# A two-layer RWKV-7 and sparse-attention kernel: the decay's first column set by VectorE, four pairs' products and the first inverses issued later, and one unit's bonus sums in another phase

## The chip, the cores and the metric

The kernel runs on one core of a Trainium2 chip. The metric is the time of one execution in microseconds (us) as the device reports it, and the median of several executions is compared. The engines are TensorE (PE; its weight loads are shown as PEld), VectorE (DVE), ScalarE (ACT), GpSimd (POOL) and SyncE (SP), which here only issues transfers. Each engine works through its own list of instructions in order, and waits at an instruction until the semaphores that it needs have been raised.

## The reference

The reference runs 256 tokens of width 2048 through two layers. The first is an RWKV-7 mixer, the second an attention layer over compressed, selected and windowed keys. The change touches the first layer alone. Cut to what matters, it computes per head of 64:

```python
kk = kk / jnp.maximum(jnp.sqrt(jnp.sum(kk * kk, axis=-1, keepdims=True)), 1e-12)
k = k * (1.0 + (a - 1.0) * k_a)

def step(S, inp):                       # over the 256 tokens
    r_t, w_t, k_t, v_t, a_t, b_t = inp
    sa = jnp.einsum('bhvk,bhk->bhv', S, a_t)
    S = S * w_t[:, :, None, :] + sa[..., None] * b_t[:, :, None, :] + v_t[..., None] * k_t[:, :, None, :]
    return S, jnp.einsum('bhvk,bhk->bhv', S, r_t)

bonus = jnp.sum((rh * kh * r_k).astype(jnp.float32), axis=-1, keepdims=True) * vh
o = (o + bonus.reshape(B, T, D)) * jax.nn.silu(z)
return o.astype(u.dtype) @ w_o, v
```

There are 32 heads, so 16 pairs of heads (128 rows, one per partition) and 8 units of two pairs.

## The kernel before

All large products are made with 32-bit numbers split in a high and a low half: ACT rounds (`whi`, L207), DVE subtracts (`wlo`, L192), and TensorE makes three matmuls for one. The weights stream through five raw buffers; their loads stand in SP's list (L179).

The recurrence over tokens is done in four chunks of 64. Inside a chunk it needs the inverse of a triangular matrix for each head, which is made in advance.

**Up to about 335 us** the projections run: values, then blocks of z (`phase_z`) and keys (`phase_k`, one for each pair) in the order z0, k0 to k7, z1, k8 to k11, z2, k12 to k15, z3. Beside them run generators, which give back a time after which they want to be continued; a small scheduler in Python (`Sched`) counts the time of the matmuls that it has emitted and continues them when due. In this part the order of each engine's list is then set once more by a list scheduler, which simulates the program and takes what is ready.

- `stage_k(j)` makes for pair j the decayed keys in the buffer `sp` (three of them): `pp` (the running decay, whose first column of every chunk is 1), `at`, `BK` and `kr`. POOL sets the first column (L758), makes a power for the norm (`rnt`, L747), which ACT spreads (`rnx`, L753) and TensorE turns (L756), and makes the products `BK` (L775, L776). DVE makes `nk`, `at` and `an` (L768 to L770). The buffer is stored to DRAM (`spd`, L778). Eight small matmuls (L784) give the matrix to be inverted; ACT copies it (L788), and SP stores it (`abdd`, L796). Pair j starts after the matrix of pair j - 2 is issued.
- `stage_t(b)` inverts the matrices of pairs 8b to 8b + 7, on DVE almost alone: it loads them (`invA`, L819), sets the diagonal of `invT` (L828), copies the first entries below it (L830), doubles the size in steps of 2 and 4 (L849 to L860) and then of 8 and 16 (L868, L873), and stores the result from POOL (L894, L900). Inverse 0 runs beside the projections, inverse 1 in the scan.

**From about 335 to 550 us** the scan runs; there all lists stand in the order of the code. For each unit U of 8 there are 12 phases: chunk c = 0 to 3, step p = 0 to 2. Step 0 makes `px` (L1105, and L1121 with the state S), which ACT copies to `X`; step 1 makes `pu` (L1128), step 2 the output and the next state (L1134, L1137), which DVE copies or adds (L1140, L1142). In between the phases TensorE makes the projection r and the output projection (`fill`; L1257 to L1259 are r's), and the next unit's preparations (A: L1088, L1090; masks on DVE: L1096; G: L1055; Y: L1064; B: L1074). The bonus sums (L1116) are 16 matmuls with a moving operand of two columns that add up `mb` over a head.

After 550 us come the key and value projections, the attention and the output; the change leaves them alone.

Of the kernel before, what the change touches and what calls it, by code (L numbers as in the profile page):

```python
# [13 lines left out]
OP = mybir.AluOpType  # L14
# [6 lines left out]
NCH = T // CH  # L21
# [197 lines left out]
def hybrid_kernel(ctx: ExitStack, tc: tile.TileContext, a: dict, out: bass.AP):  # L219
    nc = tc.nc  # L220
    V, S, G, PE = nc.vector, nc.scalar, nc.gpsimd, nc.tensor
# [36 lines left out]
    def accp(name="acc"):  # L258
        n = turn.get(name, 0)
        turn[name] = n + 1  # L260
        b = role[name]
        return psum.tile([128, 512], F32, name=f"bank{b[n % len(b)]}", bufs=1)
# [27 lines left out]
    for q in range(4):  # L290
        for k in (4 * q, 4 * q + 2):
            first, second = [W.add(wv[(k + i) * 128:(k + i + 1) * 128, 0:1024].rearrange("p (u c) -> p u c", u=2), 1, False)
                             for i in range(2)]
# [158 lines left out]
    pp = accp("pp")  # L452
# [262 lines left out]
    def stage_k(j):  # L715
        PE, V, S, G = Ranked(nc.tensor, "skPE"), Ranked(nc.vector, "skE"), Ranked(nc.scalar, "skE"), Ranked(nc.gpsimd, "skE")
        yield lambda: j in kdone and (j < KLAG or (j - KLAG) in a1done)
        tmp = lambda name, bufs=2: kph.tile([128, T], F32, name=name, bufs=bufs)
        sp = kph.tile([128, SPW], F32, name="sp", bufs=3)
        abs_ = tmp("abs")  # L720
        BK = sp[:, 0:512].rearrange("p (c x t) -> p c x t", c=NCH, x=2)
        pp = sp[:, 512:512 + NCH * (CH + 1)].rearrange("p (c t) -> p c t", c=NCH)
        kr = sp[:, SPW - 512:SPW - 256]
        at = sp[:, SPW - 256:]
        w2t = w2[j // 2]
        sc = (j % 2) * 128
        la = accp("la")
        PE.matmul(la[:, :256], w2t[:, 0, sc:sc + 128], hw, start=True, stop=True)
        PE.matmul(la[:, 256:], w2t[:, 1, sc:sc + 128], ha, start=True, stop=True)
        sch.t += 860  # L730
        pk = kps.pop(j)
        ksb = tmp("ksb")
        sqk = tmp("t1")
        S.activation(ksb, pk, AF.Copy)
        S.activation(sqk, pk, AF.Square, scale=KK[:, j:j + 1])
        rn = accp("rn")
        for tt in range(2):
            PE.matmul(rn[:, 256 + 2 * tt:258 + 2 * tt], sqk[:, tt * 128:(tt + 1) * 128], C("bo"), start=True, stop=True)
        sch.t += 430
        yield 400.0  # L740
        sst = kph.tile([128, 2, 2], F32, name="sst", bufs=2)
        rnt = kph.tile([128, 2, 2], F32, name="rnt", bufs=2)
        thw, tha = tmp("thw"), tmp("tha")
        S.activation(thw, la[:, :256], AF.Tanh, scale=0.5, bias=W0H[:, j:j + 1])
        S.activation(tha, la[:, 256:], AF.Tanh, scale=0.5, bias=A0H[:, j:j + 1])
        V.tensor_scalar(sst, rn[:, 256:260].rearrange("p (a b) -> p a b", a=2), 1e-24, None, op0=OP.max)
        G.tensor_tensor(rnt, sst, half[:, 0:4].rearrange("p (a b) -> p a b", a=2), op=OP.pow)  # L747
        S.activation(thw, thw, AF.Copy, scale=0.5, bias=0.5)
        cum = tmp("cum")
        V.tensor_tensor_scan(cum, C("rst"), thw, 0.0, op0=OP.mult, op1=OP.add)  # L750
        yield 1000.0
        rnx = tmp("rnx")
        S.activation(rnx.rearrange("p (a b n) -> p a b n", a=2, b=2),  # L753
                     rnt[:, :, :, None].to_broadcast([128, 2, 2, 64]), AF.Copy)
        for tt in range(2):
            PE.transpose(rn[:, tt * 128:(tt + 1) * 128], rnx[:, tt * 128:(tt + 1) * 128], ident)  # L756
        sch.t += 215
        G.memset(pp[:, :, 0:1], 1.0)  # L758
        S.activation(pp[:, :, 1:], c3(cum), AF.Exp, scale=-DECAY)
        pinv = tmp("pinv")  # L760
        S.activation(pinv, cum, AF.Exp, scale=DECAY)
        an, f = tmp("an"), tmp("f")
        S.activation(an, tha, AF.Copy, scale=-0.5, bias=-0.5)
        S.activation(f, tha, AF.Identity, scale=KAH[:, j:j + 1], bias=KAM[:, j:j + 1])
        V.tensor_tensor(f, ksb, f, op=OP.mult)
        yield 800.0
        nk = tmp("nk")
        V.scalar_tensor_tensor(nk, ksb, KKN[:, j:j + 1], rn[:, :256], op0=OP.mult, op1=OP.mult)  # L768
        V.tensor_tensor(c3(at), c3(nk), pp[:, :, 0:CH], op=OP.mult)
        V.tensor_tensor(an, nk, an, op=OP.mult)  # L770
        S.activation(kr, f, AF.Copy, scale=RK[:, j:j + 1])
        yield 600.0
        for h in range(2):
            r = slice(64 * h, 64 * h + 64)
            G.tensor_tensor(BK[r, :, 1 - h, :], c3(an)[r], c3(pinv)[r], op=OP.mult)  # L775
            G.tensor_tensor(BK[r, :, h, :], c3(f)[r], c3(pinv)[r], op=OP.mult)  # L776
        yield 2500.0
        nc.sync.dma_start(spd[j], sp)  # L778
        ab = [accp("ab") for _ in range(2)]
        for c in range(NCH):  # L780
            q = slice(64 * (c % 2), 64 * (c % 2) + 64)
            for h in range(2):
                r = slice(64 * h, 64 * h + 64)
                PE.matmul(ab[h][q, c // 2 * 64:c // 2 * 64 + 64], c3(at)[r, c, :], BK[r, c, 1 - h, :], start=True, stop=True)  # L784
        sch.t += 350
        blocks = abs_.rearrange("p (n s) -> p n s", s=64)
        for h in range(2):
            S.activation(blocks[:, h::2], ab[h][:, :128].rearrange("p (n s) -> p n s", s=64), AF.Copy)  # L788
        for odd in range(2):
            for q in range(2):  # L790
                d = abdd[j // 8][q]
                n = 4 * (q + 1)
                dst = bass.AP(tensor=d.tensor, offset=d.offset + (j % 8 * 2 + odd) * n * 1024, ap=[[32, 32], [1024, n], [1, 32]])
                r0 = 64 * odd + 32 * q
                src = blocks[r0:r0 + 32].rearrange("p n (e s) -> p (n e) s", e=2) if q else blocks[r0:r0 + 32, :, 0:32]
                nc.sync.dma_start(dst, src)  # L796
        a1done.add(j)
# [12 lines left out]
    def stage_t(b):  # L810
        PE, V, S, G = Ranked(nc.tensor, "stE"), Ranked(nc.vector, "stE"), Ranked(nc.scalar, "stE"), Ranked(nc.gpsimd, "stE")
# [10 lines left out]
        if b:  # L822
            yield lambda: "inv" in phase_done
            V.memset(Tm, 0.0)
        else:
            yield 500.0
        flat = Tm.rearrange("p a b -> p (a b)")
        V.memset(flat[:, 0::33], 1.0)  # L828
        fa = A.rearrange("p a b -> p (a b)")
        V.tensor_copy(flat[:, 32::66], fa[:, 32::66])  # L830
        yield 1000.0

        pace = lambda ns: PACE[0] * (ns + 60.0) if b else 1.6 * (ns + 60.0)
# [6 lines left out]
        for lv in (2, 4):  # L840
            n = 32 // (2 * lv)
            m1 = M1.rearrange("p a b -> p (a b)")[:, :n * lv * lv].rearrange("p (n i j) -> p n i j", n=n, i=lv)
            m2 = M2.rearrange("p a b -> p (a b)")[:, :n * lv * lv].rearrange("p (n i j) -> p n i j", n=n, i=lv)
            x = X[:, :n * lv * lv].rearrange("p (n i j) -> p n i j", n=n, i=lv)
            sh = [128, n, lv, lv]
            for k in range(lv):
                colA = view(A, lv, k, n, 2 * lv, lv, 1).to_broadcast(sh)
                rowT = view(Tm, k, 0, n, 2 * lv, 1, lv).to_broadcast(sh)
                V.tensor_tensor(m1 if k == 0 else x, colA, rowT, op=OP.mult)  # L849
                if k:  # L850
                    V.tensor_tensor(m1, m1, x, op=OP.add)
                yield pace((1 if k == 0 else 2) * (1.1 * n * lv * lv + 60.0))
            for k in range(lv):
                colT = view(Tm, lv, lv + k, n, 2 * lv, lv, 1).to_broadcast(sh)
                rowM = m1[:, :, k:k + 1, :].to_broadcast(sh)
                V.tensor_tensor(m2 if k == 0 else x, colT, rowM, op=OP.mult)
                if k:
                    V.tensor_tensor(m2, m2, x, op=OP.add)
                yield pace((1 if k == 0 else 2) * (1.1 * n * lv * lv + 60.0))
            V.tensor_copy(view(Tm, lv, 0, n, 2 * lv, lv, lv), m2)  # L860
# [45 lines left out]
    H = lambda x, h: R[h ^ x]  # L906
# [200 lines left out]
    def phase(U, c, p):  # L1107
        uv, px, pu, pS = UV[U % 2], view(U, 0, 64), view(U, 64, 64), view(U, 128, 64)
        O = view(U, 192 + 64 * c, 64)
        st = SST[U][0] if c else None  # L1110
        if p == 0:
            if c == 0:
                for i in range(NCH):
                    for x, h in each:
                        o = x * 512 + 448 + 2 * i
                        PE.matmul(PBK[U][H(x, h), o:o + 2], mb[R[h], x, 64 * i:64 * i + 64], ones2[R[h]], start=True, **mm)  # L1116
            removal(U, c)
            if c:
                for k, o in enumerate((px, O)):
# [796 lines left out]
```

## Time and profile before

| | us |
|---|---|
| median of three runs | 1112.94 |
| lowest and highest | 1112.37, 1113.22 |
| the profiled execution | 1114.21 |
| its span, first to last instruction | 1112.4 |

The profile is of one execution, 1.27 us over the median. Rows of the timeline give start and duration in us, then engine, line, operation, what is written and read, the shape and a count; in square brackets stands how long the engine was idle before it, and what released it. Rows of waits give the waiting engine, its tile and line, the releaser, and the total, the number and the longest in us; "issue" is a wait for nothing that the profile shows. Rows by windows give for each stretch and engine the busy time and the number of instructions, then the clock that TensorE was granted, the busy share of the 16 transfer engines, and GB/s. A matmul with 32-bit operands that are not split shows twice, so the 16 of the bonus sums are 32 rows of the trace and 32 weight loads.

### The profile page before, as it was taken

To read this page: it belongs to the slowest core of one execution; us is meant where nothing else is said; L and a number is where in the kernel's file an instruction comes from. 1 tells how busy PE (TensorE), PEld (TensorE's weight loads), DVE (VectorE), ACT (ScalarE), POOL (GpSimd) and SP (SyncE) were. 2 spreads that over 40 slices of the span, in tenths; PEclk is the share of its full clock that TensorE was granted. 3 is DMA by queue.
4 is the path that set the end of the run, shared out by engine and by line. 5 is a ranking of instruction groups with operands and counts; after the bars stand their busy time and mean duration, and the time that the engine had idled before them with its cause. 6 is when DMAs were issued, how large, how long until landed. Compare 5 with 4: busy or idle time off the path is not lost.

```text
span 1112.4 us, 25288 instructions
## 1 busy us (share of the span) xinstructions
PE 1091.2 (98%) x9232; PEld 957.1 (86%) x9232; DVE 836.1 (75%) x1784; ACT 737.7 (66%) x1779; POOL 329.6 (30%) x409
## 2 busy tenths in 40 slices
PE   8999999999999999999999999999999999999997
PEld 7788899898889888999888888788989999988887
DVE  6999976779887796666667876665677988886564
ACT  7767877676775467776557766665666677775553
POOL 1300035424448456652200110100323324432012
PEclk9999999999999999999999999999999999999999
DMA  7458978877879777865578668675745354735762
GB/s 260 152 194 235 248 212 249 247 197 216 260 222 269 223 194 211 245 197 156 160 250 277 197 203 260 195 253 169 198 139 152 101 145 131 187 103 194 281 199 100
DMA packets 221965, 224.74 MB, mean 202 GB/s; under 512 B 48368, under 2 KB 173392, under 8 KB 221456
## 3 DMA queue, kind: packets, MB, share of 16 engines
q1 hardware_dynamic: 216512, 217.60, 66.1%
q0 software_dynamic: 4864, 4.92, 1.6%
q8 instruction: 73, 1.20, 0.4%
q10 hardware_dynamic: 464, 0.59, 0.1%
q14 instruction: 52, 0.43, 0.1%
HBM read 200.49 MB, written 22.58 MB: 201 GB/s over the span
## 4 chain that ended last, share of the span: by engine, by line
PE 54%; DVE 4%; DMA 2%; issue 1%; ACT 1%; POOL 0%; POOLq 0%; DVEq 0%; ACTq 0%
PE bank L619 9%; PE bank L617 9%; PE bank L616 9%; PE bank L1657 5%; PE bank L235 4%; PE bank L1658 3%; DVE wlo L192 2%; PE bank L1257 1%; PE pair L619 1%; PE pair L616 1%; PE pair L617 1%; PE bank L1258 1%; PE bank L1259 1%; PE bank L1223 1%; PE pair L1134 1%
## 5 line engine op out<-in xcount | busy, mean ns | idle before, releaser
L192 DVE TENSOR_TENSOR wlo<-wraw,whi 128x512 fp32r<-128x512 f32 (+2 forms) x616 | 440.3, 728 | 144.0 <-ACT whi L207 139.7
L207 ACT ACTIVATE whi<-wraw 128x512 fp32r<-128x512 f32 (+2 forms) x664 | 401.8, 618 | 179.5 <-PE bank L619 69.6
L192 POOL TENSOR_TENSOR wlo<-wraw,whi 128x512 fp32r<-128x512 f32 (+2 forms) x48 | 61.4, 1279 | 174.3 <-ACT whi L207 134.9
L617 PE MATMUL bank<-wlo,mh 128*128 128x512 f32 (+1 forms) x288 | 109.4, 381 | 0.8 <-DVE wlo L192 0.7
L617 PE MATMUL bank<-wlo,mhl 128*128 128x512 f32 (+2 forms) x288 | 107.9, 375 | 0.0
L619 PE MATMUL bank<-whi,ml 128*128 128x512 f32 (+1 forms) x288 | 107.9, 379 | 0.0
L619 PE MATMUL bank<-whi,mhl 128*128 128x512 f32 (+2 forms) x288 | 107.3, 373 | 0.0
L616 PE MATMUL bank<-whi,mhl 128*128 128x512 f32 (+2 forms) x288 | 99.5, 373 | 0.3 <-ACT Vt L1539 0.3
L616 PE MATMUL bank<-whi,mh 128*128 128x512 f32 (+1 forms) x288 | 92.0, 381 | 0.3 <-ACT whi L207 0.2
L1657 PE MATMUL bank<-mhl,whi 128*128 128x512 f32 x256 | 91.9, 397 | 0.0
L1257 PE MATMUL bank<-mhl,whi 128*128 128x256 f32 x256 | 78.6, 307 | 2.0 <-issue 2.0
L617 PE MATMUL bank<-wlo,kvh 128*128 128x512 f32 x192 | 76.0, 396 | 0.0
L634 PE MATMUL bank<-mh,whi 128*128 128x256 f32 x256 | 75.2, 294 | 0.4 <-ACT whi L207 0.4
L619 PE MATMUL bank<-whi,kvl 128*128 128x512 f32 x192 | 75.3, 392 | 0.0
L636 PE MATMUL bank<-mh,wlo 128*128 128x256 f32 x256 | 73.7, 290 | 0.0
L635 PE MATMUL bank<-ml,whi 128*128 128x256 f32 x256 | 73.4, 287 | 0.0
L1658 PE MATMUL bank<-mhl,wlo 128*128 128x256 f32 x256 | 73.0, 285 | 0.3 <-DVE wlo L192 0.3
L1259 PE MATMUL bank<-mhl,wlo 128*128 128x256 f32 x256 | 72.7, 284 | 0.1
L1258 PE MATMUL bank<-mhl,whi 128*128 128x256 f32 x256 | 72.7, 284 | 0.0
L616 PE MATMUL bank<-whi,kvh 128*128 128x512 f32 x192 | 66.7, 391 | 0.0
L617 PEld LDWEIGHTS bank<-wlo,mh 128*128 128x128 f32 x288 | 54.1, 188 | 11.5 <-DVE wlo L192 2.0
L619 PEld LDWEIGHTS bank<-whi,ml 128*128 128x128 f32 x288 | 54.2, 188 | 9.6
(384 smaller groups left out, 2746.4 us busy)
## 6 DMA issues: line engine op xcount, KB each, us to landing
wraw<-in_a_w_rkvz_dram SPq DMA_DIRECT2D x128, 512.0 KB, 5.1
wraw<-in_kv_w_dram SPq DMA_DIRECT2D x48, 512.0 KB, 4.4
wraw<-in_b_w_in_dram SPq DMA_DIRECT2D x40, 512.0 KB, 4.3
wraw<-in_a_w_o_dram SPq DMA_DIRECT2D x32, 512.0 KB, 4.9
wraw<-in_b_w_o_dram SPq DMA_DIRECT2D x32, 512.0 KB, 3.7
spd<-sp SPq DMA_DIRECT2D x16, 642.0 KB, 4.7
wraw<-in_b_w_in_dram SPq DMA_DIRECT2D x24, 384.0 KB, 3.2
wraw<-in_cmp_w_dram SPq DMA_DIRECT2D x16, 512.0 KB, 3.9
```

Source lines behind the costliest of these rows:

```text
L192: eng.tensor_tensor(lv, src, hv.bitcast(F32), op=OP.subtract)
L207: self.nc.scalar.activation(hv, src, AF.Copy)
L616: PE.matmul(o, mh[:, ts], wh[:, 0, :], start=k == ends[0], stop=False)
L617: PE.matmul(o, mh[:, ts], wl[:, 0, :], start=False, stop=False)
L619: PE.matmul(o, ml[:, ts], wh[:, 0, :], start=False, stop=k == ends[1])
L634: PE.matmul(o, wh[:, s, :], mh, start=k == 0 and first, stop=False, **kw)
L636: PE.matmul(o, wl[:, s, :], mh, start=False, stop=k == NK - 1, **kw)
L1257: PE.matmul(oo, wh[:, i, c], mh, start=k == 0 and x == 0, stop=False, **kw)
L1258: PE.matmul(oo, wh[:, i, c], ml, start=False, stop=False, **kw)
L1259: PE.matmul(oo, wl[:, i, c], mh, start=False, stop=k == NK - 1, **kw)
L1657: PE.matmul(o, wh[:, s, :], beside[("u", k)], start=k == 0, stop=False)
L1658: PE.matmul(o[:, :T], wl[:, s, :], mh, start=False, stop=k == NK - 1)
```

## The change

Five edits. In `stage_k` the first column of the decay is set by DVE instead of POOL and stands after `nk`, held in the program's order; the store of `sp` is issued before the pause ahead of the matrix products, not after it; and that pause is 9.5 us instead of 2.5 for pairs 8 to 11. In `stage_t` inverse 0 pauses 18 us instead of 0.5 before its first steps, and its first copy (now ahead of the diagonal) and its products of size 2 are held in the program's order. In `phase` the first unit's bonus sums are issued at the start of phase (1, 2), the sixth, and add to what stands there (`start=False`); those of the other units stay in phase (0, 0).

```diff
@@ stage_k
-        G.memset(pp[:, :, 0:1], 1.0)
         S.activation(pp[:, :, 1:], c3(cum), AF.Exp, scale=-DECAY)
...
         V.scalar_tensor_tensor(nk, ksb, KKN[:, j:j + 1], rn[:, :256], op0=OP.mult, op1=OP.mult)
+        tc.keep_in_program_order(V.memset(pp[:, :, 0:1], 1.0))
         V.tensor_tensor(c3(at), c3(nk), pp[:, :, 0:CH], op=OP.mult)
...
-        yield 2500.0
         nc.sync.dma_start(spd[j], sp)
+        yield 9500.0 if 8 <= j < 12 else 2500.0
@@ stage_t
         else:
-            yield 500.0
+            yield 18000.0
         flat = Tm.rearrange("p a b -> p (a b)")
+        fa = A.rearrange("p a b -> p (a b)")
+        first = V.tensor_copy(flat[:, 32::66], fa[:, 32::66])
+        if not b:
+            tc.keep_in_program_order(first)
         V.memset(flat[:, 0::33], 1.0)
-        fa = A.rearrange("p a b -> p (a b)")
-        V.tensor_copy(flat[:, 32::66], fa[:, 32::66])
...
-                V.tensor_tensor(m1 if k == 0 else x, colA, rowT, op=OP.mult)
+                first = V.tensor_tensor(m1 if k == 0 else x, colA, rowT, op=OP.mult)
+                if lv == 2 and not b:
+                    tc.keep_in_program_order(first)
...
-                V.tensor_tensor(m2 if k == 0 else x, colT, rowM, op=OP.mult)
+                first = V.tensor_tensor(m2 if k == 0 else x, colT, rowM, op=OP.mult)
+                if lv == 2 and not b:
+                    tc.keep_in_program_order(first)
@@ phase
+        if (c, p) == ((0, 0) if U else (1, 2)):
+            for i in range(NCH):
+                for x, h in each:
+                    o = x * 512 + 448 + 2 * i
+                    PE.matmul(PBK[U][H(x, h), o:o + 2], mb[R[h], x, 64 * i:64 * i + 64], ones2[R[h]], start=U > 0, **mm)
         if p == 0:
-            if c == 0:
-                for i in range(NCH):
...
             removal(U, c)
```

In the changed kernel the lines of this part have other numbers: `f` is L764, `nk` L767, the memset L768, the inverse's first copy L829 and its products of size 2 L851 and L860, r's matmuls L1263 to L1265, the bonus sums L1121.

How the lists of the engines differ is shown at three places. The first is POOL's list at the third to fifth pair of the keys, before and now:

```order
L747 TENSOR_TENSOR rnt<-sst,half 128x4
L758 MEMSET sp 128x4
L775 TENSOR_TENSOR sp<-an,pinv 64x4x64 x2
L776 TENSOR_TENSOR sp<-f,pinv 64x4x64 x2
L747 TENSOR_TENSOR rnt<-sst,half 128x4
L758 MEMSET sp 128x4
L775 TENSOR_TENSOR sp<-an,pinv 64x4x64 x2
```

```order
L747 TENSOR_TENSOR rnt<-sst,half 128x4
L775 TENSOR_TENSOR sp<-an,pinv 64x4x64 x2
L776 TENSOR_TENSOR sp<-f,pinv 64x4x64 x2
L747 TENSOR_TENSOR rnt<-sst,half 128x4
L775 TENSOR_TENSOR sp<-an,pinv 64x4x64 x2
```

The memsets are gone, and the products stand directly behind the power; the order of the rest is the same.

The second is the start of inverse 0, around the end of z1. DVE's list before, from a pair's `an` on:

```order
L770 TENSOR_TENSOR an<-nk,an 128x256
L192 TENSOR_TENSOR wlo<-wraw,whi 128x512 x8
L830 COPY invT<-invA 128x16
L849 TENSOR_TENSOR invM<-invA,invT 128x32
L849 TENSOR_TENSOR invX<-invA,invT 128x32
L192 TENSOR_TENSOR wlo<-wraw,whi 128x512
```

and now:

```order
L770 TENSOR_TENSOR an<-nk,an 128x256
L192 TENSOR_TENSOR wlo<-wraw,whi 128x512 x11
L691 TENSOR_TENSOR zth<-bank_2798,zth 128x512
L691 TENSOR_TENSOR zth<-bank_2799,zth 128x512
L192 TENSOR_TENSOR wlo<-wraw,whi 128x512
L829 COPY invT<-invA 128x16
L192 TENSOR_TENSOR wlo<-wraw,whi 128x512
L851 TENSOR_TENSOR invM<-invA,invT 128x32
```

The copy stands six rows later (four `wlo`, and z1's two products). On TensorE the eight matmuls of pair 8 (L784) stand 25 places later: behind the 1399th matmul of the list, not the 1374th, and behind the transposes of pair 9:

```order
L756 MATMUL bank_3303<-cst,rnx 128x128 x2
L634 MATMUL bank_3286<-mh,whi 128x256
L635 MATMUL bank_3286<-ml,whi 128x256
L636 MATMUL bank_3286<-mh,wlo 128x256
L784 MATMUL bank_3449<-sp 64x64
L784 MATMUL bank_3450<-sp 64x64
```

Those of pairs 9 and 10 stand 19 and 4 places later, those of pair 11 where they stood.

The third is the first unit's scan on TensorE. Before, at phase (0, 0):

```order
L1259 MATMUL bank_4693<-mhl,wlo 128x256
L1116 MATMUL pair_5093<-ones_4712,mb 64x2 x16
L1105 MATMUL pair_5093<-uv_4697,ama_4699 64x64 x4
L1257 MATMUL bank_4693<-mhl,whi 128x256
L1258 MATMUL bank_4693<-mhl,whi 128x256
```

and now, at phase (1, 2):

```order
L1061 MATMUL pair_5208<-Yb_4696,a_4559 64x32 x16
L1134 MATMUL pair_5093<-X,Yb_4560 64x64 x4
L1080 MATMUL bank_4692<-cst,spl_4695 128x128 x3
L1070 MATMUL pair_5208<-gs,t_4561 64x32 x16
L1121 MATMUL pair_5093<-ones_4712,mb 64x2 x16
L1140 MATMUL pair_5093<-uv_4697,amr_4701 64x64 x4
```

The sums now stand between the second unit's Y (L1070) and the output of the first unit's second chunk (L1140).

More of the change, by code (lines that the diff above doesn't have):

```diff
@@ L1110, in phase @@
         st = SST[U][0] if c else None
-        if p == 0:
-            if c == 0:
-                for i in range(NCH):
-                    for x, h in each:
-                        o = x * 512 + 448 + 2 * i
-                        PE.matmul(PBK[U][H(x, h), o:o + 2], mb[R[h], x, 64 * i:64 * i + 64], ones2[R[h]], start=True, **mm)
+        if (c, p) == ((0, 0) if U else (1, 2)):
[3 more added lines that the diff above has]
+                    PE.matmul(PBK[U][H(x, h), o:o + 2], mb[R[h], x, 64 * i:64 * i + 64], ones2[R[h]], start=U > 0, **mm)
+        if p == 0:
             removal(U, c)
```

## The prediction

> **What bounds the kernel now.** I read the page first, then who waited for whom, then short windows around the waits.
>
> ```profile
> PE 1091.2 (98%) x9232; PEld 957.1 (86%) x9232; DVE 836.1 (75%) x1784; ACT 737.7 (66%) x1779; POOL 329.6 (30%) x409
> ```
>
> TensorE is busy 98% of the span of 1112.4 us, so the change, which removes no matmul, can gain only from TensorE's idle time and slow time. These are the waits of TensorE that it can touch (total us, times, longest).
>
> ```profile
> PE bank L784 <- POOL sp L775: 2.1, 4, 0.7
> PE bank L1257 <- issue: 2.0, 1, 2.0
> PE bank L756 <- ACT rnx L753: 0.7, 1, 0.7
> PE bank L1090 <- issue: 0.7, 1, 0.7
> ```
>
> Together 5.5 us. Slow time shows in windows of 3.41 us (the granted clock stands behind POOL, ahead of the DMA share):
>
> ```profile
> core 0: us, PE busy (x) PEld busy (x) DVE busy (x) ACT busy (x) POOL busy (x), PEclk, DMA share, GB/s
> 244.65:248.06 3.41, 2.10 (x27) 1.69 (x26) 3.41 (x10) 1.29 (x4) 2.50 (x3) 1.00 0.49 158
> 248.06:251.47 3.41, 3.41 (x14) 3.23 (x15) 3.31 (x8) 2.99 (x8) 2.66 (x3) 0.50 0.92 297
> ...
> 360.70:364.11 3.41, 1.39 (x47) 1.30 (x46) 3.20 (x13) 0.80 (x2) 0.83 (x2) 1.00 1.03 283
> 364.11:367.53 3.42, 3.42 (x21) 3.08 (x21) 3.18 (x13) 0.78 (x3) 2.04 (x3) 0.50 1.12 308
> ...
> 370.94:374.35 3.41, 3.41 (x119) 2.90 (x119) 1.33 (x7) 2.58 (x8) 1.15 (x3) 1.00 0.94 284
> ```
>
> Twice a window in which TensorE did little (2.10 and 1.39 us busy) is followed by one at a clock of 0.50. The price of a slow window comes from the pace of like matmuls, full and slow:
>
> ```profile
> 238.08 0.28 PE L634 MATMUL bank<-mh,whi 128*128 128x256 f32 x1
> 238.20 0.28 PE L635 MATMUL bank<-ml,whi 128*128 128x256 f32 x1
> ...
> 248.59 0.41 PE L635 MATMUL bank<-ml,whi 128*128 128x256 f32 x1
> 248.80 0.41 PE L636 MATMUL bank<-mh,wlo 128*128 128x256 f32 x1
> ```
>
> 0.12 us from start to start against 0.21: a slow window loses 3.41 x (1 - 0.12/0.21) = 1.46 us. Both slow windows follow waits of the list above, so a wait there costs more than its length.
>
> [...]
>
> **Part 1: the first column's memset leaves POOL.** POOL is served in order.
>
> ```profile
> 171.90 0.42 DVE L770 TENSOR_TENSOR an<-nk,an 128x256 f32<-128x256 f32 x1
> ...
> 174.18 0.10 POOL L758 MEMSET sp<- 128x4 f32 x1 [5.07 <-DMA spd<-sp]
> ...
> 177.76 1.01 POOL L747 TENSOR_TENSOR rnt<-sst,half 128x4 f32<-128x4 f32 x1
> ...
> L758 POOL MEMSET sp<- x16: 100/105/108, 124.5 to 310.6; 128x4 f32 x16
> ...
>   DMA spd<-sp: 22.9, 8
> ...
> 355.46 0.09 DVE L828 MEMSET invT<- 128x32 f32 x1
> ```
>
> The memset belongs to a later pair than the products behind it, and waits 5.07 us for that pair's buffer to be stored, while the input of the products (`an`) is ready at 172.3. The products, the L784 matmuls and, through the late `rnt`, the L756 transposes wait for it: 0.7 us and one of the four L784 waits. All such waits of POOL are 22.9 us in 8 times, and leave with the memset. On DVE it stands behind `nk`, when ACT and POOL have long written the same buffer; it waits for nothing new. Its price is bounded by 0.105 us on POOL and the smallest DVE memset here, 0.09: 16 x 0.09 = 1.4 us of DVE in 200 us, of which 0.4 falls in the crowded stretch below.
>
> **Part 2: first inverses and products of pairs 8 to 11 later.**
>
> ```profile
> 227.52 1.15 ACT L690 ACTIVATE zth<-zth 128x512 f32<-128x512 f32 x2
> ...
> 228.29 0.18 DVE L830 COPY invT<-invA 128x16 f32<-128x16 f32 x1 [4.53 <-DMA invA<-abdd]
> ...
> 244.66 0.42 DVE L770 TENSOR_TENSOR an<-nk,an 128x256 f32<-128x256 f32 x1
> 245.15 2.31 POOL L775 TENSOR_TENSOR sp<-an,pinv 64x256 f32<-64x256 f32 x2 [4.13 <-DVE an L770]
> 246.38 0.45 PE L784 MATMUL bank<-sp 64*64 64x64 f32 x8 [0.63 <-POOL sp L775]
> ...
> 228.29:289.81 61.52, 58.56 (x132) 0.97 0.77 213
> 289.81 0.69 DVE L192 TENSOR_TENSOR wlo<-wraw,whi 128x512 fp32r<-128x512 f32 x1 [1.77 <-ACT whi L207]
> SPq L778 <- POOL sp L775: 9.6, 3, 3.8
> ```
>
> DVE stands 4.53 us for a load, and everything queued behind it is late for 60 us: DVE is busy 58.56 of 61.52 us until it is idle again (1.77 us at 288). Pair 8's `an` comes at 245.08, POOL's products end at 247.46, and TensorE, due at 245.75 (246.38 less 0.63), waits twice. Now the copy stands behind six more rows, the last the z products. Their input is ready at 228.67; two products and one `wlo` at 0.6 to 0.7 each put the copy at 230.6, 2.3 us later than before. But the six rows that stood behind it (some 4 us at 0.69) are then done: DVE's list is 4.0 - 2.3 = 1.7 us ahead (between 0, if inputs hold the rows up, and 4.53). Pair 8's chain also stands ahead of the inverse's wide rows, and its matmuls come 25 places later, 3 us at 0.12. So POOL is done ahead of TensorE, and the waits and the first slow window go.
>
> With part 1 this is 2.1 + 0.7 + 1.46 = 4.26 us. TensorE then runs 3.2 us earlier through this stretch (4.26 less the 1.1 of part 1), against 1.7 + 1.77 = 3.5 us that DVE has to give: just enough. I take off 0.7 us for waits that come into sight when TensorE is earlier (between 0 and 1.5): **3.5 us**.
>
> The stores of `sp` stand ahead of the yield, so SP blocks earlier on POOL; its longest such wait was 3.8 us, against five raw buffers of weights that are loaded ahead. I cost it at nothing; if that cover were gone, part of a 3.8 us wait would show on ACT's `whi`.
>
> **Part 3: the bonus sums of the first unit.**
>
> ```profile
> 361.26 0.64 PE L1116 MATMUL pair<-ones,mb 64*64 64x2 f32 x32
> 361.75 0.32 PE L1105 MATMUL pair<-uv,ama 64*64 64x64 f32 x8
> 364.10 0.37 PE L1257 MATMUL bank<-mhl,whi 128*128 128x256 f32 x1 [2.02 <-issue]
> ...
> q8 instruction: 73, 1.20, 0.4%
> ...
> q1 hardware_dynamic: 514, 1.41, 103.0%
> ...
> q8 instruction: 1, 0.02, 2.8%
> ...
> q8 instruction: 1, 0.02, 5.4%
> ```
>
> At 362 TensorE waits 2.02 us for no semaphore. Queue q8 moves 1.20 MB in 73 packets for some 2 x 9232 TensorE instructions: about 253 a packet. The last three rows are of the DMA view of 357.3 to 361.3 (no q8 packet; q1 alone fills the engines), 361.3 to 364.1 (one) and 368.5 to 370 (the next). So I read the gap as TensorE out of instructions: short matmuls, the sums' 64 instructions among them (32 matmuls, 32 weight loads), use up a block faster than the queue, crowded by q1, brings the next. Without the 64 the same block lasts through 21 wide matmuls and L1128, over 2.5 us more at 0.12 each; the 2.02 us go, and with them the second slow window: 3.48 us at most.
>
> But DVE does not let all of it through.
>
> ```profile
> 367.74 0.28 DVE L868 TENSOR_TENSOR invX<-invA,invM 128x128 f32<-128x128 f32 x1
> 369.38 0.29 DVE L1140 COPY S<-pair 128x128 f32<-128x128 f32 x1 [1.36 <-PE pair L1137]
> ...
> 371.26 0.41 PE L1121 MATMUL pair<-S,ars 64*64 64x64 f32 x16
> ...
> 372.82 0.67 PE L1064 MATMUL pair<-gs,t 64*64 64x32 f32 x32
> ```
>
> The state copy L1140 stands behind inverse steps that end at 368.02. It waited 1.36 us for TensorE; it can come no more than that earlier, so L1121, which reads it, starts at 368.3 at best: 2.9 us earlier. The next instruction block arrives by 370 and, as after the gap, some 1.4 us later it is usable: 371.4. It is needed after L1064, which ends at 373.4 now and would at 370.5: 0.9 us are lost again. Then the moved sums cost their 0.49 us (361.26 to 361.75) in the sixth phase. 2.9 - 0.9 - 0.5 = **1.5 us**, between 0 (or a loss of 1.5, when the new waits make a slow window) and 3.5.
>
> [...]
>
> **Sum.** 3.5 + 1.5 = 5.0 us. The profiled execution took 1114.21, 1.8 over its span and 1.27 over the median of 1112.94; from its own time 1109.2, in terms of the median **1107.9 us**.
>
> **The rivals.**
> - *Part 3 gives nothing.* The block is late whatever stands in it, or the wait comes back at the next block and L1121 and makes a new slow window (the window from 370.94, all short matmuls, has little work even without a wait). For it: L1090 shows a second issue wait, 0.7 us, with no sums near. Against it: q8's late packet. 1112.94 - 3.5 = 1109.4.
> - *Everything comes through.* New waits stay at 0 and DVE lets 3.48 pass: 4.26 + 3.48 = 7.7, 1105.2. Against it: the 1.36 us.
> - *The waits move.* Pairs 10 and 11 or `whi` make TensorE wait instead, with one slow window: only the 1.1 us of part 1 and some tenths remain: 1111.6. For it: ACT and DVE are shared by weights, pairs and inverses.
> - *Slower: DVE's list ends too late.* If the six rows gain nothing, the list ends 2.3 us later while TensorE is 3.2 us earlier: 2.3 + 3.2 - 1.77 = 3.7 us of waits for `wlo` in the z rows around 285, in three places, each with a slow window (4.4): 1.1 + 3.2 - 3.7 - 4.4 = -3.8, 1116.7. It decides once those waits exceed 4.3 us. Against it: 4.53 us of dead time are gone.
>
> **How the numbers follow.** Forecast 0.41, part 3 nothing 0.17, everything 0.10, waits move 0.19, slower 0.13. 0.2% (2.2 us) is about what a measurement tells from no change. The first three are faster: 0.68; same 0.19; slower 0.13. The range 1104.9 to 1111.9 holds all cases but the slower one and some tails.
>
> **What would show it.** POOL without waits for `spd` before memsets; no wait of 4.5 us at the first copy of the inverse, and no L784 wait after 200 us; no window at 0.50 between 240 and 260; L1140 without a wait for TensorE and L1121 waiting for it. I am wrong if L617 or L784 waits for DVE or POOL around 280 us, or if a gap without a releaser and a clock of 0.50 stand anywhere between 355 and 385.

## The result, and the profile after

The changed kernel takes 1107.50 us, the median of six executions (1107.31 to 1109.61), against 1113.95 us for six of the kernel before (1112.37 to 1116.32). The ratio is 0.9944, with a 95% interval from 0.9928 to 0.9961: 6.2 us faster, between 4.3 and 8.0. The forecast was 5.0 us, at 1107.9. The sum came out, but neither of the two terms that it was added up from did, as the parts below show. The page of the changed kernel begins like this (busy us, share of the span, instructions):

```profile
span 1107.4 us, 25278 instructions
...
PE 1089.3 (98%) x9232; PEld 955.8 (86%) x9232; DVE 836.2 (76%) x1800; ACT 736.4 (66%) x1779; POOL 327.8 (30%) x393
```

TensorE executes the same instructions in 5.0 us less of span, and is as full as before. The profiled execution took 1109.2 us, one of the two longer ones of the six. The waits of TensorE that the change touches, in the same view as before (total us, times, longest):

```profile
PE pair L1134 <- ACT X L1129: 1.7, 3, 0.7
...
PE pair L1111 <- DVE S L1146: 1.0, 1, 1.0
...
PE bank L634 <- ACT whi L207: 0.7, 1, 0.7
...
PE bank L756 <- ACT rnx L753: 0.5, 1, 0.5
PE bank L636 <- DVE wlo L192: 0.4, 1, 0.4
```

The four L784 waits (2.1 us) and the two "issue" waits (2.0 and 0.7) are gone. Most of the L756 wait has stayed, 0.5 of 0.7. In their place stand a wait of the scan for VectorE's state copy (L1111, 1.0), a third wait of L1134 (before: L1128) for `X`, and 0.4 us for `wlo`. Now the windows, with the columns of the prediction's table:

```profile
core 0: us, PE busy (x) PEld busy (x) DVE busy (x) ACT busy (x) POOL busy (x), PEclk, DMA share, GB/s
244.50:247.90 3.40, 3.40 (x44) 3.27 (x42) 3.24 (x10) 2.63 (x6) 2.42 (x3) 1.00 0.91 264
247.90:251.30 3.40, 3.40 (x33) 2.89 (x24) 3.33 (x12) 3.03 (x10) 0.69 (x1) 1.00 0.54 176
363.22:366.64 3.42, 2.03 (x81) 1.69 (x83) 3.11 (x14) 2.45 (x9) 0.56 (x1) 1.00 1.05 301
366.64:370.05 3.41, 3.41 (x84) 3.28 (x77) 0.66 (x4) 1.51 (x6) 2.41 (x5) 0.50 0.86 249
370.05:373.46 3.41, 3.41 (x37) 3.12 (x36) 2.27 (x8) 0.73 (x2) 1.70 (x5) 0.50 0.78 182
```

Around 248 us TensorE is full and the clock is 1.00. Around 366 us there are now two windows at 0.50 in a row, where one stood before.

Where the time went can be read by pairing the same TensorE instruction in two traces: how much earlier it starts in the other kernel, less what the two traces already differ by at 150 us (0.04 to 0.8 us). The columns are places in the kernel before; negative is later. At 288 and 291 us the rows without the late inverse and without the late products have some instructions of TensorE in another order. All kernels of this document are in it, for the experiments below.

| TensorE earlier than in the kernel before, us, at | 200 | 288 | 291 | 345 | 395 |
|---|---|---|---|---|---|
| the changed kernel | 1.0 | 5.4 | 4.7 | 4.4 | 4.0 |
| the changed kernel, second trace | 1.0 | 5.4 | 4.7 | 4.4 | 6.6 |
| part 1 alone | 1.0 | 1.9 | 1.9 | -1.1 | -0.5 |
| part 2 alone | -0.4 | 4.0 | 3.2 | 2.9 | 3.9 |
| parts 1 and 2 | 1.0 | 5.4 | 4.8 | 4.5 | 5.8 |
| part 3 alone | -0.4 | -0.2 | -0.2 | -0.2 | -0.6 |
| the change without the late inverse | 1.0 | -0.2 | -0.2 | -1.1 | -1.6 |
| the change without the late products | 1.0 | 4.5 | 4.1 | 3.3 | 4.2 |
| the kernel before with idle matmuls | 0.1 | -0.2 | -0.2 | -0.2 | -1.4 |
| the change with the state copy first | 1.0 | 5.4 | 4.7 | 4.4 | 7.2 |
| the same, second trace | 1.0 | 5.4 | 4.7 | 4.4 | 6.2 |
| the same without part 3 | 1.0 | 5.4 | 4.7 | 4.4 | 6.0 |
| part 3 and the state copy first, without parts 1 and 2 | -1.2 | -1.8 | -1.8 | -1.9 | -1.2 |

Up to 345 us every kernel with parts 1 and 2 in full gives the same 4.4 us, to 0.1. The program of the kernel before scatters more: three rows (part 3 alone, the idle matmuls, part 3 and the state copy first) have its lists up to 345 us, and are 0.2, 0.2 and 1.9 us later there. In the 50 us behind that, the start of the scan, two traces of one and the same kernel differ by 2.6 us.

### The profile page after: what moved, and what is told of

It is laid out like the page before. It is cut to its first block, busy times and chain, and to the rows that moved or that the text cites. A ratio compares the mean times of both kernels' runs of the same rounds, so it can differ in the third digit from the quotient of the medians.

```text
span 1107.4 us, 25278 instructions
## 1 busy us (share of the span) xinstructions
PE 1089.3 (98%) x9232; PEld 955.8 (86%) x9232; DVE 836.2 (76%) x1800; ACT 736.4 (66%) x1779; POOL 327.8 (30%) x393
## 4 chain that ended last, share of the span: by engine, by line
PE 56%; DVE 4%; ACT 2%; issue 1%; DMA 0%; SPq 0%; POOLq 0%; POOL 0%; DVEq 0%; ACTq 0%
PE bank L616 9%; PE bank L617 9%; PE bank L619 9%; PE bank L1663 5%; PE bank L235 4%; PE bank L1664 3%; PE bank L1263 2%; DVE wlo L192 2%; PE pair L619 1%; PE pair L616 1%; PE bank L1264 1%; PE bank L1265 1%; PE pair L617 1%; PE bank L1229 1%; PE pair L1140 1%
## 5 line engine op out<-in xcount | busy, mean ns | idle before, releaser
L1263 PE MATMUL bank<-mhl,whi 128*128 128x256 f32 x256 | 78.8, 308 | 0.0
L1265 PE MATMUL bank<-mhl,wlo 128*128 128x256 f32 x256 | 72.9, 285 | 0.1
L1264 PE MATMUL bank<-mhl,whi 128*128 128x256 f32 x256 | 72.8, 284 | 0.0
L776 POOL TENSOR_TENSOR sp<-f,pinv 64x256 f32<-64x256 f32 x32 | 29.4, 919 | 121.3 <-DVE f L764 110.2
```

Of the source, the lines that this page charges most:

```text
L1263: PE.matmul(oo, wh[:, i, c], mh, start=k == 0 and x == 0, stop=False, **kw)
L1264: PE.matmul(oo, wh[:, i, c], ml, start=False, stop=False, **kw)
L1265: PE.matmul(oo, wl[:, i, c], mh, start=False, stop=k == NK - 1, **kw)
```

## The experiments

Theory at the outset: VectorE's list up to 290 us is the cap of the projections, part 2 lifts it, part 1 adds what POOL was late; part 3 removes a stop of TensorE for a block of instructions and is then held up by the state copy. Rivals: each part gains on its own what TensorE waited for it; the later products, not the later inverse, carry part 2; the stop at 362 us has another cause; part 3 gives nothing.

**Part 1 alone.**

```diff
-        G.memset(pp[:, :, 0:1], 1.0)
...
+        tc.keep_in_program_order(V.memset(pp[:, :, 0:1], 1.0))
         V.tensor_tensor(c3(at), c3(nk), pp[:, :, 0:CH], op=OP.mult)
```

> The kernel before with the first column of the decay set by VectorE, and nothing else; the lists of TensorE, ScalarE and SyncE stay as they were. Theory (the parts add up, and each gains what TensorE waited for it): TensorE is 1.1 us earlier from 178 us on (0.7 us of L756 and about 0.4 us of one L784), the waits of L784 at 245.5, 247 and 282 us and both windows at 0.50 stay; 1.1 us off the time, ratio about 0.999. Rival (an earlier POOL also serves the crowded stretch): the L784 waits after 200 us shrink too and the gain is 2 to 4 us.

Ratio 1.0008 [0.9998, 1.0019]: no gain at all. TensorE is 1.0 us earlier at 200 us as expected, and 1.9 at 291. Then it stops. In this kernel's rows stand TensorE's wait, the inverse step on VectorE that is late (L873) and the ScalarE copy that waits for it (L898), and the windows:

```profile
PE bank L634 <- DVE wlo L192: 1.6, 1, 1.6
```

```profile
285.35 1.21 DVE L873 TENSOR_REDUCE invT<-invX 128x64 f32<-128x1024 f32 x1
...
286.59 1.27 ACT L898 ACTIVATE invA<-invT 128x256 f32<-128x256 f32 x2 [2.51 <-DVE invT L873]
```

```profile
290.60:294.01 3.41, 1.72 (x11) 1.11 (x10) 3.41 (x7) 3.41 (x9) 0.00 (x0) 1.00 1.05 318
294.01:297.42 3.41, 3.41 (x18) 3.41 (x18) 1.59 (x4) 2.61 (x7) 3.00 (x3) 0.50 0.76 174
```

L873 starts at 285.35 us; before it was 285.65. VectorE's list moved by 0.3 us where TensorE moved by 1.9. ScalarE waits twice as long for it (2.51 us, before 1.26), the `whi` behind it are late, and TensorE waits 1.6 us with a window at 0.50 behind that. Both my theory here ("the parts add up") and its rival fall: the 1.9 us won ahead of VectorE's full list came back here as a wait of 1.6 us, and with the slow window, in this trace, as more than it was: TensorE is 1.1 us later at 345 us. The rival had one thing right: the L784 waits after 200 us shrank from 1.7 to 0.9 us, and no window at 0.50 stands behind them, against what I expected.

**Part 2 alone** is the change without its memset lines and with the bonus sums in phase (0, 0).

> The kernel before with part 2 alone: the store of sp ahead of the pause, the pause of 9.5 us for pairs 8 to 11, the first inverse 18 us later; the first column stays on POOL and the bonus sums stay in phase (0, 0). Theory: the L784 waits at 245 to 283 us and the first window at 0.50 go (0.63 + 0.69 + some 0.6 + 1.46 = 3.4 us), about 0.8 us come back as waits for whi and wlo around 285 us, so TensorE is 2.5 to 3.5 us earlier at 300 us; the wait of 2 us at 362 us stays. Ratio 0.997 to 0.998. Rival (the two parts need each other, since POOL is blocked by its memsets for the very pairs that are moved): under 1.5 us at 300 us.

Ratio 0.9966 [0.9955, 0.9978], 3.8 us faster; 2.9 us at 345 us. The wait at 362 us stayed, now 1.1 us long. Part 2 is the part that stands by itself.

**Parts 1 and 2 without part 3.**

```diff
-        if (c, p) == ((0, 0) if U else (1, 2)):
+        if (c, p) == (0, 0):
```

(with `start=True` for all units, as before).

> The changed kernel with the bonus sums back in phase (0, 0), so parts 1 and 2 together. Theory: TensorE is 4.5 us earlier at 350 us as in the changed kernel, and the gap of some 2 us behind L1105 is there again, 4.5 us earlier, as is a window at 0.50 behind it; time 4 to 4.6 us under the kernel before, 0.5 to 2.5 us over the changed kernel. Rival (part 3 does nothing that parts 1 and 2 had not done already): no gap, and the time of the changed kernel.

Ratio 0.9952 [0.9938, 0.9965], 5.4 us faster. The gap and the window at 0.50 are back, as expected, at 357.8 and 360.5 us; the time is 0.9 us over the changed kernel's by the ratios, well inside the intervals. Part 1, worth nothing alone, is worth 1.6 us at 345 us behind part 2 (4.5 against 2.9).

**Part 3 alone** is the same edit the other way, on the kernel before.

> The kernel before with part 3 alone: the first unit's bonus sums in phase (1, 2); nothing ahead of 361 us differs. Theory (TensorE out of instructions): the gap of 2.0 us without a releaser at 362 us goes; L1121 waits for DVE's state copy, which moves at most 1.36 us; a window at 0.50 may come back in the stretch of short matmuls behind it; 0 to 2 us off the time. Rival (the gap is not a matter of instructions): the gap stays behind L1105 and the time is the same or up to 0.5 us worse.

Ratio 0.9999 [0.9986, 1.0012]. The gap is gone, and the last of the wide matmuls ahead of the next L1105 starts 3.8 us earlier (367.07 us, before 370.88); by 376 us all of it is lost again, in these rows of waits and windows:

```profile
PE pair L1105 <- DVE S L1140: 1.0, 1, 1.0
```

```profile
366.73:370.15 3.42, 1.83 (x66) 1.52 (x68) 3.25 (x14) 1.79 (x6) 0.48 (x1) 1.00 1.10 311
370.15:373.56 3.41, 3.41 (x83) 2.95 (x85) 0.69 (x4) 1.91 (x6) 1.00 (x3) 0.50 1.07 343
373.56:376.97 3.41, 3.41 (x27) 3.29 (x24) 2.24 (x8) 1.11 (x3) 3.18 (x8) 0.50 0.34 74
```

First comes the wait for the state copy, then one for `X`, then two windows at half clock; short matmuls fill the first.

The same trace tells something of part 2, since up to 350 us its lists are those of the kernel before. TensorE waits for POOL at 246 and 247 us as before (0.51 and 0.69 us), but the edge of a window falls into the second wait, and no window at 0.50 follows:

```profile
243.86:247.27 3.41, 2.52 (x25) 2.17 (x24) 3.05 (x9) 1.98 (x5) 1.99 (x2) 1.00 0.64 210
247.27:250.68 3.41, 3.11 (x26) 2.85 (x27) 3.38 (x9) 2.61 (x8) 3.00 (x4) 1.00 0.70 198
```

TensorE is 1.3 us ahead of the kernel before at 255 us. At 267.7 us it waits for POOL once more (0.52 us), and at 285 us it is 0.2 us behind. Being spared the slow window at 248 us was worth nothing here by 285 us.

**Which half of part 2: the inverse back to its old time, and the products back to theirs.**

```diff
-            yield 18000.0
+            yield 500.0
```

> The changed kernel with the first inverse's pause back at 0.5 us (its copies and products of size 2 still held in the program's order). Theory (VectorE's list is the cap of this stretch, and only the later inverse moves it): VectorE stands 4 us or so for the load of invA again, its list up to 290 us ends as late as before, and what TensorE wins ahead of 285 us it gives back there as a wait for whi or wlo with a window at 0.50, as in the run with the memset alone; the gain over the kernel before falls from 6 us to between 0 and 2. Rival (the later products carry part 2): 4 to 6 us remain.

```diff
-        nc.sync.dma_start(spd[j], sp)
-        yield 9500.0 if 8 <= j < 12 else 2500.0
+        yield 2500.0
+        nc.sync.dma_start(spd[j], sp)
```

> The changed kernel with the pause of 2.5 us ahead of the products of all pairs and the store of sp behind it, as before; the inverse stays late. Theory (VectorE's list is the cap): most of the gain stays, 4 to 6 us under the kernel before; at most one or two waits of L784 for POOL, under 1 us together, show between 240 and 285 us. Rival (the later products carry part 2): the L784 waits at 245 and 282 us and the window at 0.50 behind them stay, and no more than 2.5 us of gain remain.

Without the late inverse the ratio is 0.9991 [0.9976, 1.0005], without the late products 0.9944 [0.9928, 0.9960], the changed kernel's own. So the later inverse carries part 2; the later products and the earlier store show no share in the time. VectorE's row of the kernel without the late inverse:

```profile
227.81 0.18 DVE L829 COPY invT<-invA 128x16 f32<-128x16 f32 x1 [4.79 <-DMA invA<-abdd]
```

and of the changed kernel:

```profile
228.62 0.68 DVE L192 TENSOR_TENSOR wlo<-wraw,whi 128x512 fp32r<-128x512 f32 x1
229.22 0.17 DVE L829 COPY invT<-invA 128x16 f32<-128x16 f32 x1
```

From 222 to 290 us VectorE is busy 60.41 us in the former,

```profile
222.00:290.00 68.00, 60.41 (x140) 1.00 0.74 209
```

and 63.92 us in the latter:

```profile
222.00:290.00 68.00, 63.92 (x146) 1.00 0.76 222
```

The 4.79 us of standing still have become 3.5 us of work. Without that work done early TensorE's waits for `whi`, `wlo` and `rnx` come to 3.6 us in 245 to 296 us, and a window at 0.50 stands behind.

**Is the stop at 362 us a missing block of instructions?** Sixteen idle matmuls, 64 TensorE instructions, are put into the kernel before at 350 us, 12 us ahead of the stop, so that a stop that keeps to a count of instructions comes 64 instructions earlier in the program.

```diff
     PBK[1] = pair_tile(1)
+    for i in range(16):
+        r = R[i % 2]
+        PE.matmul(PBK[1][r, 1020:1022], ident[r, r], ones2[r], start=True, **mm)
```

> The kernel before with 16 idle matmuls more (64x64 of the identity by a column pair, 64 TensorE instructions, into columns that nothing reads) at about 349 us, ahead of the first unit's preparations, and nothing else. Theory (a block of 256 instructions has not come): the gap without a releaser stands 64 instructions earlier in the program than in the kernel before, ahead of the bonus sums and not behind L1105, again at the same count modulo 256 of TensorE's instructions, 1 to 2.5 us long; the 0.7 us gap inside L1090 at 383 us moves 64 instructions earlier too or goes. Time 0 to 1 us longer. Rival (the gap belongs to the first wide matmul behind L1105, by its operands or its bank): the gap stays behind L1105 at 2 us.

The gap stands in the middle of the bonus sums, whose operands have all been there:

```profile
362.51 0.33 PE L1116 MATMUL pair<-ones,mb 64*64 64x2 f32 x9
364.06 0.53 PE L1116 MATMUL pair<-ones,mb 64*64 64x2 f32 x20 [1.22 <-issue]
```

Counted along TensorE's rows (matmuls, weight loads and its 190 semaphore rows) it is at the 5057th again, as in the kernel before, where another instruction stood there (r's L1257, stopped for 2.02 us). The other stop of the kernel before, L1090's 0.7 us, is at the 5825th row, 768 or 3 x 256 rows on. The same count modulo 256, 193, holds for three more stops that this kernel has and the kernel before has not (the 6849th, 7873rd and 8897th):

```profile
PE pair L1206 <- issue: 2.8, 2, 1.4
...
PE pair L1116 <- issue: 1.2, 1, 1.2
PE bank L1258 <- issue: 0.8, 1, 0.8
```

So these six stops of two traces keep to the count, whatever instruction stands there. That a block of 256 instructions ends at such a count, and that the next one comes late, is my reading; why TensorE stops at one such place and not at another was not tested. Below, a place at 193 modulo 256 is called an edge. I had the time wrong, 0 to 1 us: it is 1.0020 [1.0005, 1.0036], 2.2 us slower for 16 tiny matmuls. In the trace three more stops stand further on (1.4, 1.4 and 0.8 us); that these make the 2.2 us was not tried by itself.

**Is it the state copy that hides part 3?** The second inverse's steps on VectorE are spaced wider during the first unit's phases 0 to 2 and closer afterwards, so that the first state copy (L1146) stands ahead of six more of them.

```diff
-        PACE[0] = PACES[min(U + 1, 3)]
+        PACE[0] = PACES[min(U + 1, 3)] if U else 4.0
...
-                PACE[0] = PACES[1]
+                PACE[0] = 1.2
```

> The changed kernel with the second inverse's steps spaced wider in the first unit's phases 0 to 2 (4.0 for 1.8 times their length) and closer from there on (1.2 for 1.8), so that the first state copy stands ahead of six more of them and the list has caught up by 385 us; VectorE's order alone differs. Theory (behind part 3 TensorE waits for the state copy): L1111 waits under 0.3 us for it in place of 1.0, the copy X in front of L1134 follows, the window at 0.50 from 366.6 us goes or is half as long; 0.5 to 3 us under the changed kernel. Rival (the stretch of short matmuls is itself too little work for the full clock, or the block of instructions behind L1070 is late next): the window at 0.50 stays and the time is within 0.7 us of the changed kernel.

Ratio 0.9921 [0.9909, 0.9933]; the wait of L1111 is gone, and so is the window at 0.50. That looked like a version to keep, and like the proof of the theory. The last group was to settle it on one chip: the changed kernel and this version again, this version without part 3, and part 3 with this edit on the kernel before.

> The changed kernel once more, beside the three that follow on the same chip: 0.994 to 0.995 of the kernel before; a wait of L1111 for the state copy of about 1 us.

> The changed kernel with the second inverse's steps spaced so that the first state copy stands ahead of them, once more. Theory (what TensorE wins in part 3 the late state copy takes back): 1.5 to 3 us under the changed kernel of the same call, ratio to the kernel before 0.991 to 0.993. Rival (the lead of the first time was scatter): within 0.7 us of the changed kernel.

> The version with the state copy first, but the bonus sums back in phase (0, 0). Theory (the sums in phase (0, 0) use up the block of instructions, and the state copy hides what moving them is worth): the gap without a releaser of some 1.4 us behind L1105 is there with a window at 0.50 behind it in most runs, 1.5 to 3.5 us over the version with the state copy first. Rival (only the state copy counts, part 3 gives nothing): within 0.7 us of it.

> The kernel before with part 3 and with the state copy first, without parts 1 and 2. Theory: part 3, which alone gave nothing, now shows: no gap at 362 us, no wait of L1105 for the state copy, 2 to 3.5 us under the kernel before, ratio 0.997 to 0.998. Rival (part 3 pays only behind parts 1 and 2): ratio 0.999 to 1.001.

| on one chip, against the kernel before | ratio | 95% interval |
|---|---|---|
| the changed kernel | 0.9951 | 0.9936 to 0.9967 |
| with the state copy first | 0.9945 | 0.9930 to 0.9959 |
| the same without part 3 | 0.9938 | 0.9926 to 0.9950 |
| part 3 and the state copy first, without parts 1 and 2 | 0.9997 | 0.9984 to 1.0010 |

The theory fell. With the state copy out of the way part 3 still gives nothing that shows (0.9945 against 0.9938 without it; 0.9997 on the kernel before, where the trace has neither the gap at the 5057th row nor the wait for the state copy, but a new wait of 1.5 us for POOL's `ars`, L1044), and the lead of the version over the changed kernel did not come again. The traces say why in part. With the state copy first TensorE goes on to later edges and stops there; this is the second trace of that version:

```profile
PE pair L1134 <- ACT X L1129: 1.6, 3, 0.6
...
PE pair L1134 <- issue: 1.0, 1, 1.0
...
PE pair L1070 <- issue: 0.5, 1, 0.5
```

and this the version without part 3, where the gap among r's matmuls behind L1111 is back:

```profile
PE bank L1264 <- issue: 1.2, 1, 1.2
...
PE pair L1134 <- ACT X L1129: 1.0, 2, 0.5
...
PE pair L1134 <- issue: 0.4, 1, 0.4
```

One edge is the same in both (the 5825th row); the other is the 5313th with part 3 and the 5057th without. That is 1.5 and 1.6 us of "issue" in all: in these two traces part 3 only chooses at which edges TensorE waits. I know no version from these runs that is measurably faster than the changed kernel.

## Why the prediction was right, and where it was wrong

- **Part 1, 1.1 us: right in size, wrong as a term that stands alone.** TensorE was 1.0 us earlier at 200 us in every kernel with it, mostly through the first L784 (0.8) and little through L756 (0.1), which still waits 0.5 us. POOL has no memset left to wait ahead of. The memset costs VectorE 62 ns, under both of my bounds (90 and 105). But without part 2 it returns everything at 291 us; the rival "the waits move" left it 1.1 us, and that was wrong too.
- **Part 2: the mechanism was right, the size too small.** The copy of the inverse came at 229.22 us with no wait, where I had 230.6 on the clock of the kernel before, some 229.6 with part 1; the L784 waits and the slow window at 248 us went; the waits around 285 us that a rival named are there, but small (0.4 for `wlo`; 0.7 for `whi`, of which the kernel before has 0.4). Parts 1 and 2 together were to give 3.5 us; they gave 4.4 at 345 us. The mis-sized term is the 4.26: TensorE got 5.4 us ahead by 288 us, and 1.0 came back by 345 us, against 4.26 and 0.7 forecast. What VectorE had to give was more than "just enough": from 222 to 290 us it does 63.92 us of work, and 59.84 in the kernel before. The 4.26 is also not three prices that add up. Its 1.46 us for the slow window at 248 us belongs to the profiled execution: the trace of part 3 alone, with the same lists up to 350 us, has a clock of 1.00 from 243.86 to 250.68 us and was 0.2 us behind at 285 us.
- **The products 9.5 us later, the store ahead of the pause:** costed at nothing for the store, and as the thing that puts POOL ahead of TensorE for the products. The run without both has no L784 wait after 200 us either (its trace loses 1 us to a window at 0.50 at 291 us, behind a wait of 0.9 us for `whi`, which its times do not show as a loss). POOL was late because VectorE was; the later place was not needed.
- **Part 3, 1.5 us: wrong.** The step that failed is "The next instruction block ... 0.9 us are lost again" together with the end of the sum, "2.9 - 0.9 - 0.5". The 2.9 us up to the state copy nearly came true (L1111's first chain with the state starts 7.1 us earlier than before, of which 4.4 are parts 1 and 2 and 2.7 are left), and L1146 no longer waits while L1111 does. But what lies behind it took all of it and not half: not a stop for the next block, which I had priced at 0.9 us (neither trace of the changed kernel has a stop without a releaser), but a wait for `X` (0.65 us), and in the first trace two windows at half clock. With the state copy first, stops at the 5313th and 5825th row stand there (0.5 and 1.0 us). I had the loss of 1.5 us by a new slow window as a bound, and its rival "part 3 gives nothing" at 0.17; by four comparisons that rival is the one that happened (by the ratios 0.1, 0.3 and 0.9 us for part 3 and 0.8 against it; taken singly most of them leave room for 1.5 us, together they centre near nothing). Of my sign of being wrong, a gap without a releaser and a clock of 0.50 between 355 and 385 us, the second half stood in the very first trace; the gap did not.
- **The sum** came out by luck: parts 1 and 2 gave more than I gave them, and part 3 less, and the two errors cancelled. Beyond the 4.4 us the times show about 1 us more (5.4 by the ratio of parts 1 and 2 alone). Where that is stays open: behind 345 us the traces scatter by more than it, and the one trace of the kernel before that the table compares with is the earliest of four with its program at 345 us.

Stops without a releaser are few. TensorE's rows reach an edge 73 times in the trace of the kernel before and 73 times in that of the changed kernel; the first has a stop at two of them, the second at none. Those that show are not all small: in six traces the rows of waits have one of 1.1 to 2.0 us at L1257, L1264 or L1116.

## What to carry to other kernels

Before a stall is booked as a gain, look for the engine whose list is full behind it: 1.9 us won ahead of it came back as a loss of 1.1, and the same edit was worth 1.6 us once that engine's own standing still had been filled with work. A slow window of one trace is not yet a price: another trace with the same lists up to 350 us went without the window at 248 us and was 0.2 us behind at 285 us. Time a version more than once, on one chip, before explaining its lead: one kernel gave 0.9921 and then 0.9945, both with narrow intervals. When other instructions are moved to a stop without a releaser, see whether it keeps its count: here it stood at the 5057th row again (2.02 us, then 1.22), so it was not the wait of the instruction that stood there; and with the state copy first, with the sums moved past it, a stop showed at the 5313th instead (0.5 us).

## What was unexpected in the hardware

**The grid of the clock.** The windows at 0.50 of one trace lie on a grid of 3.413 us: in the kernel before they start at 248.06 and 364.11 us, 34 steps apart, in the kernel with idle matmuls at 364.32 and 436.00 us, 21 steps apart. The grid lies at another offset from the program's start in other traces (the start of such a window less whole steps): 2.3 us in the kernel before, 1.4 in the changed kernel, 0.5 with part 1 alone, 2.8 without the late inverse. In the traces of the kernel before and of the changed kernel, three of some 626 windows at full clock between 20 and 1095 us held less than 2.7 us of TensorE work (2.10, 1.39 and 2.03); each was followed by a window at 0.50, and no other was. In the rows by windows of eight more kernels ten such windows held 1.72 to 2.40 us of work. Seven were followed by a window at 0.50 and three were not (2.06 us at 269.05 us without the late inverse, 2.40 at 362.67 without the late products, 2.25 at 357.73 with the state copy first and without part 3), while without the late products one followed a window with 2.81 us of work. None of these windows was idle; the least work was 1.39 us. The same waits can so be cut by the grid in two: in the second trace of the changed kernel the wait of L1111 is as long as in the first (1.0 us), but falls like this,

```profile
360.73:364.14 3.41, 2.43 (x44) 2.15 (x42) 3.24 (x14) 0.32 (x2) 1.51 (x3) 1.00 1.13 275
364.14:367.55 3.41, 2.75 (x131) 2.39 (x125) 2.06 (x9) 2.98 (x11) 0.90 (x2) 1.00 0.96 295
```

and no slow window follows. Between these two traces of one kernel that is 2.6 us at 395 us (4.0 and 6.6 in the table). The times agree: of the twelve executions of the changed kernel, the four with a mean granted clock of 0.995 took 1109.2 us or more, and the eight with 0.997 or more took 1108.7 us or less. That a cluster of waits costs a slow window with a chance that depends on how it meets the grid is my reading of these rows; it was not tried by itself.

**Two slow windows in a row.** In the changed kernel the window at 0.50 from 366.64 us is followed by another, and so is the one from 370.15 us with part 3 alone; in the kernel before neither is (248.06 and 364.11 us). Behind 366.64 us in the changed kernel TensorE is "busy" 3.41 of 3.41 us at half clock, first with short matmuls, then mostly with r's wide ones, and the next window is at 0.50 too. The row of busy time does not tell why: at the 0.21 us from start to start that wide matmuls took at 0.50, about 16 of them fill a window of 3.41 us, against about 28 at the 0.12 us of the full clock.
